# Cross-attention of a hybrid decoder trunk: the logits of heads 0 and 1 traced between the two halves of the second token tile's query projection

## The chip, the core and the metric

The kernel runs on one core of one Trainium2 chip. The metric is device time in microseconds (us) of one execution, and the median of several runs is given. The engines are named as in the profile: PE (TensorE, matmul; PEld its weight load), ACT (ScalarE), DVE (VectorE), POOL (GpSimd) and SP (SyncE, which issues the DMAs).

## What is computed

The reference is a trunk of four layers over a residual stream of 256 tokens with 1024 features. Each layer has a token mixer (convolution, dilated attention or RWKV-7), a cross-attention into 256 memory tokens with 4 heads of 256 features, and a squared-ReLU MLP; after each part comes `x = LayerNorm(alpha * x + part(x))`. The change lies in the cross-attention and in a helper that the MLP uses too:

```python
def memory_cross_attention(x, mem, w_q, w_kv, w_out):
    q = (x @ w_q).reshape(b, s, XATTN_HEADS, XATTN_HEAD_DIM)
    kv = (mem @ w_kv).reshape(b, mem.shape[1], 2, XATTN_HEADS, XATTN_HEAD_DIM)
    logits = jnp.einsum('bshe,bmhe->bhsm', q, kv[:, :, 0]) * (XATTN_HEAD_DIM ** -0.5)
    p = jax.nn.softmax(logits, axis=-1)
    o = jnp.einsum('bhsm,bmhe->bshe', p, kv[:, :, 1])
    return o.reshape(b, s, D_MODEL) @ w_out
def sq_relu_mlp(x, w1, w2):
    return jnp.square(jax.nn.relu(x @ w1)) @ w2
```

## The kernel before

Large products run as three matmuls of rounded parts. A weight chunk of 128x1024 comes by DMA from SP into `ws` (3 buffers), ACT rounds it into `wh` (a cast, L138), DVE computes the rest into `wl` (L139); `wh` and `wl` have 9 buffers each. A chunk's `ws` buffer is taken by the next DMA only when both have read it. This is `chunk`, L130 to L140. Activations are kept in the same two parts, transposed, as `xth` and `xtl`.

PSUM has three rings of 128x512 tiles: `psA` (4, L112), `psB` (2) and `psT` (2, for transposes). The 256 tokens are two tiles of 128, t = 0 and t = 1.

`xattn` (L329) runs once per layer, in four layers (0 to 3). Its steps:

- L372 loads the eight chunks of the query weights. `first_rows` (L198) multiplies token tile t with them into two `psA` tiles, the first and the second half (512 features, which are two heads each) of the queries. For t = 0 both halves advance together. For t = 1 the first half is finished, then the second: 24 matmuls each (L171).
- L378: for each half ACT copies the `psA` tile to SBUF, PE transposes it in four pieces (L213), and DVE copies the result into the per-head query tiles (L381).
- `scores(h)` (L338): four matmuls of the query tile with the keys `kt` into a `psA` tile (L343; fp32, and the profile records two matmuls for each), then DVE's maximum (L347) and scaling (L348), ACT's two exponentials (L352), DVE's reciprocal (L353) and two normalisations (L356).
- `values(h)` (L359): PE transposes the weights of the softmax, ACT copies them to SBUF (L363), four matmuls with the values `vt` go into a `psB` tile (L367), and ACT and DVE split the result into the two parts (L152, L153).
- `project` (L390) loads the eight chunks of the output weights (`x_w_out`) and multiplies; `norm` follows. The MLP's weights (`m_w`) come after these in SP's queue.

The program is traced from these calls and a scheduler then places the instructions in one queue per engine, each worked off in its order. The place in a queue is therefore not the place in the source. The MLP (L393) calls `first_rows` too, at L423, with ACT's relu and square (L425, L426) and four transposes for each half.

Of the kernel before, what the change touches and what calls it, by code (L numbers as in the profile page):

```python
# [23 lines left out]
NT = S // P  # L24
# [4 lines left out]
XH = 4  # L29
# [55 lines left out]
class Trunk:  # L85
# [112 lines left out]
    def first_rows(self, xt, t, ws):  # L198


        out = [self.A(), self.A()]
        if t == 0:
            self.gemm_tok(xt, t, ws, out)
        else:
            for j in range(2):
                self.gemm_tok(xt, t, [[a[:, j * 512:(j + 1) * 512] for a in w] for w in ws], out[j:j + 1])
        return out

    def transposes(self, src4):

# [118 lines left out]
    def xattn(self, layer, kv, xt, xt_out):  # L329
        nc, v, t_ = self.nc, self.nc.vector, self.t  # L330
        kt, vt = kv
        gb = self.load_gb(layer, 1)
        sc = XE ** -0.5
        oxt = self.xt()
        v3 = lambda a: a.rearrange("p (a b) -> p a b", a=2)
        qs, pts = {}, {}

        def scores(h):  # L338
            q = v3(qs.pop(h))
            sp = self.A()  # L340
            for t in range(NT):
                for e in range(2):
                    nc.tensor.matmul(sp[:, t * S:(t + 1) * S], q[:, e, t * P:(t + 1) * P], kt[:, 2 * h + e, :],  # L343
                                     start=e == 0, stop=e == 1)
            mx = self.sm.tile([P, 2], F32, name="mx", tag="mx")
            den = self.sm.tile([P, 2], F32, name="den", tag="den")
            v.tensor_reduce(out=mx, in_=v3(sp), axis=AX.X, op=OP.max)  # L347
            v.tensor_scalar(mx, mx, -sc, None, op0=OP.mult)  # L348
            p_ = self.g2()
            for t in range(NT):  # L350
                o = slice(t * S, (t + 1) * S)
                nc.scalar.activation(p_[:, o], sp[:, o], AF.Exp, bias=mx[:, t:t + 1], scale=sc, accum_out=den[:, t:t + 1])  # L352
            v.reciprocal(den, den)  # L353
            for t in range(NT):
                o = slice(t * S, (t + 1) * S)
                v.tensor_scalar(p_[:, o], p_[:, o], den[:, t:t + 1], None, op0=OP.mult)  # L356
            pts[h] = p_

        def values(h):  # L359
            p_ = pts.pop(h)  # L360
            pt = self.transposes([p_[:, (2 * t + m) * P:(2 * t + m + 1) * P] for m in range(NT) for t in range(NT)])
            pT = v3(self.g2())
            nc.scalar.copy(out=pT, in_=v3(pt))  # L363
            op = self.B()
            for c in range(2):
                for m in range(NT):
                    nc.tensor.matmul(op[:, c * S:(c + 1) * S], vt[:, m, (2 * h + c) * P:(2 * h + c + 1) * P],  # L367
                                     pT[:, m, :], start=m == 0, stop=m == 1)
            self.split(oxt[0][:, 2 * h:2 * h + 2, :], oxt[1][:, 2 * h:2 * h + 2, :], v3(op))

        w = t_["x_w_q"][layer]
        ws = [self.rows(w, k) for k in range(KC)]  # L372
        for h in range(XH):
            qs[h] = self.g2()
        for t in range(NT):
            for i, ps in enumerate(self.first_rows(xt, t, ws)):
                q = self.g2()
                nc.scalar.copy(out=q, in_=ps)  # L378
                pt = self.transposes([q[:, c * P:(c + 1) * P] for c in range(4)])
                for h in range(2):  # L380
                    v.tensor_copy(v3(qs[2 * i + h])[:, :, t * P:(t + 1) * P], v3(pt[:, h * 256:(h + 1) * 256]))  # L381
        scores(0)
        scores(1)
        values(0)
        scores(2)
        values(1)
        scores(3)
        values(2)
        values(3)
        self.project(oxt, t_["x_w_out"][layer], gb, xt_out)  # L390


# [1009 lines left out]
```

## Time and profile before

| | us |
|---|---|
| median of 3 runs (2051.99 to 2065.83) | 2058.36 |
| the profiled execution: its own time | 2057.95 |
| the profiled execution: its span | 2056.2 |
| PE busy in the span | 1944.8 |
| DVE busy | 1302.7 |
| ACT busy | 996.1 |

The span is what the trace covers, from the first to the last instruction; the execution's own time is 1.75 us longer. Mean granted TensorE clock: 0.972 of full speed. In timelines a row gives the start, the time, engine, line, operation, tiles and count, and in brackets the engine's idle time just before with the instruction that ended it. In the chain of waits a row gives start, time and the work that the chain ran through.

The four cross-attentions stand at about 213 to 250, 774 to 812, 1364 to 1402 and 1804 to 1841 us of the span.

### The profile page before, as it was taken

The numbers are of one execution on the slowest core, as the hardware profiler recorded it, in microseconds if no ns is written. First come the engines' busy times: TensorE is split into PE (matmuls) and PEld (weight loads), VectorE is DVE, ScalarE is ACT, GpSimd is POOL, SyncE is SP. The second block draws the span as 40 slices with busy tenths as digits, with TensorE's granted clock in tenths as the row PEclk, the third lists the DMA queues.
The fourth block names the chain that finished last, engine by engine and source line by source line (L and its number), as shares of the span: only waits on it lengthen the run. The fifth ranks groups of instructions, "written<-read, shape, count | busy, mean of one in ns | idle before, by whom it ended". The sixth has DMA issues, their size and how long they took to land.

```text
span 2056.2 us, 33010 instructions
## 1 busy us (share of the span) xinstructions
PE 1944.8 (95%) x13027; PEld 1716.0 (83%) x13027; DVE 1302.7 (63%) x2524; ACT 996.1 (48%) x1551; POOL 264.9 (13%) x160
## 2 busy tenths in 40 slices
PE   7999999998999999999999989989999898999998
PEld 7998779977999977798888777767898787878996
DVE  3986675454555564755575767776554499667544
ACT  4546445543554533555345634333555355545552
POOL 6960000000000000000011312100000663000000
PEclk9999999998999999999999989999999999999999
DMA  7644447656656533576655334344666441445662
GB/s 228 195 154 145 146 147 232 186 163 186 169 147 175 155 117 112 188 221 186 181 160 169 102 103 118 113 138 129 198 199 188 160 144 52 138 139 179 213 188 78
DMA packets 259739, 325.75 MB, mean 158 GB/s; under 512 B 25701, under 2 KB 219965, under 8 KB 259584
## 3 DMA queue, kind: packets, MB, share of 16 engines
q1 hardware_dynamic: 258432, 322.59, 50.8%
q8 instruction: 102, 1.67, 0.3%
q10 hardware_dynamic: 1152, 1.05, 0.2%
q14 instruction: 53, 0.43, 0.1%
HBM read 315.67 MB, written 6.88 MB: 157 GB/s over the span
## 4 chain that ended last, share of the span: by engine, by line
PE 68%; DVE 15%; DMA 6%; ACT 5%; issue 4%; POOL 1%; SPq 0%; DVEq 0%; ACTq 0%; POOLq 0%
PE psA L171 25%; PE psB L183 19%; PE psB L648 7%; PE psB L195 6%; DVE g L528 3%; DVE wl L139 3%; PE psT L213 3%; ACT wh L138 2%; DMA ws<-in_m_w_dram 2%; PE psB L367 2%; POOL wl L139 1%; DMA ws<-in_x_w_out_dram 1%; DVE x L269 1%; DVE bnst L270 1%; DMA ws<-in_x_w_kv_dram 1%
## 5 line engine op out<-in xcount | busy, mean ns | idle before, releaser
L138 ACT CAST wh<-ws 128x1024 fp32r<-128x1024 f32 x546 | 571.4, 1050 | 664.5 <-PE psA L171 167.0
L139 DVE TENSOR_TENSOR wl<-ws,wh 128x1024 fp32r<-128x1024 f32 (+1 forms) x462 | 568.7, 1234 | 421.4 <-ACT wh L138 418.5
L183 PE MATMUL psB<-xth,wh 128*128 128x256 f32 x1280 | 369.1, 289 | 9.4 <-ACT xth L152 3.7
L183 PE MATMUL psB<-xth,wl 128*128 128x256 f32 x1280 | 367.0, 287 | 7.7 <-DVE wl L139 7.7
L183 PE MATMUL psB<-xtl,wh 128*128 128x256 f32 x1280 | 366.6, 286 | 0.0
L183 PEld LDWEIGHTS psB<-xth,wh 128*128 128x128 f32 x1280 | 249.8, 195 | 14.0 <-ACT xth L152 4.1
L139 POOL TENSOR_TENSOR wl<-ws,wh 128x1024 fp32r<-128x1024 f32 x84 | 211.0, 2536 | 380.9 <-ACT wh L138 372.7
L183 PEld LDWEIGHTS psB<-xth,wl 128*128 128x128 f32 x1280 | 249.5, 195 | 8.9 <-DVE wl L139 8.6
L183 PEld LDWEIGHTS psB<-xtl,wh 128*128 128x128 f32 x1280 | 249.7, 195 | 2.3 <-issue 0.2
L171 PE MATMUL psA<-wh,xth 128*128 128x512 f32 x496 | 180.2, 406 | 3.5 <-ACT xth L152 3.0
L171 PE MATMUL psA<-wl,xth 128*128 128x512 f32 x496 | 177.1, 400 | 0.0
L171 PE MATMUL psA<-wh,xtl 128*128 128x512 f32 x496 | 175.9, 399 | 0.0
L171 PE MATMUL psA<-wh,hth 128*128 128x512 f32 x512 | 163.7, 396 | 0.0
L171 PE MATMUL psA<-wh,htl 128*128 128x512 f32 x512 | 163.3, 395 | 0.0
L171 PE MATMUL psA<-wl,hth 128*128 128x512 f32 x512 | 162.3, 393 | 0.0
L528 DVE SCALAR_TENSOR_TENSOR psA<-chp,ccols,psA 128x256 f32<-128x256 f32 x280 | 119.1, 481 | 3.0 <-PE psA L512 0.4
L171 PEld LDWEIGHTS psA<-wh,xth 128*128 128x128 f32 x496 | 94.8, 193 | 25.2 <-ACT xth L152 7.1
L171 PEld LDWEIGHTS psA<-wl,hth 128*128 128x128 f32 x512 | 96.5, 188 | 22.9
L171 PEld LDWEIGHTS psA<-wh,htl 128*128 128x128 f32 x512 | 96.2, 188 | 22.0
L895 POOL MEMSET rH<- 128x512 f32 x1 | 0.5, 528 | 869.6 <-DVE bnst L270 869.6
L171 PEld LDWEIGHTS psA<-wl,xth 128*128 128x128 f32 x496 | 94.9, 192 | 19.0
L171 PEld LDWEIGHTS psA<-wh,xtl 128*128 128x128 f32 x496 | 94.6, 191 | 18.9 <-DVE xtl L153 0.2
(326 smaller groups left out, 3568.2 us busy)
## 6 DMA issues: line engine op xcount, KB each, us to landing
ws<-in_m_w_dram SPq DMA_DIRECT2D x256, 512.0 KB
ws<-in_b_w_qkv_dram SPq DMA_DIRECT2D x72, 512.0 KB
ws<-in_x_w_kv_dram SPq DMA_DIRECT2D x64, 512.0 KB
ws<-in_a_w_in_dram SPq DMA_DIRECT2D x32, 512.0 KB
ws<-in_x_w_q_dram SPq DMA_DIRECT2D x32, 512.0 KB
ws<-in_x_w_out_dram SPq DMA_DIRECT2D x32, 512.0 KB
ws<-in_c_w_rkv_dram SPq DMA_DIRECT2D x24, 512.0 KB
ws<-in_a_w_out_dram SPq DMA_DIRECT2D x16, 512.0 KB
```

Source lines behind the costliest of these rows:

```text
L138: nc.scalar.copy(out=h[:rows], in_=f[:rows])
L139: self.lo_eng.tensor_tensor(l[:rows], f[:rows], h.bitcast(F32)[:rows], op=OP.subtract)
L171: nc.tensor.matmul(ps[j], l, r[:, j * 512:(j + 1) * 512], start=first and k == 0 and i == 0, stop=last and k == n - 1 and i == 2)
L183: nc.tensor.matmul(ps[:, c * S + toks.start:c * S + toks.stop], l, r, start=k == 0 and i == 0, stop=k == KC - 1 and i == 2)
L195: nc.tensor.matmul(ps[:, m * 256:(m + 1) * 256], l, r[:, k % 4, :], start=k == 0 and i == 0, stop=k == KC - 1 and i == 2)
L213: self.pe_last = self.nc.tensor.transpose(pt[:, i * P:(i + 1) * P], b, self.ident).ins
L269: v.scalar_tensor_tensor(xs, xs, ALPHA, ps[j], op0=OP.mult, op1=OP.add)
L270: v.bn_stats(st[:, j, :], xs)
L367: nc.tensor.matmul(op[:, c * S:(c + 1) * S], vt[:, m, (2 * h + c) * P:(2 * h + c + 1) * P], pT[:, m, :], start=m == 0, stop=m == 1)
L528: v.scalar_tensor_tensor(dst[:, o], hp[:, c, k:k + S], dwc(k, cc), src[:, o], op0=OP.mult, op1=OP.add)
L648: nc.tensor.matmul(ps, l[:, k, :], r[:, k, :], start=k == 0 and i == 0, stop=k == KC - 1 and i == 2)
L895: nc.gpsimd.memset(H, 0.0)
```

## The change

`first_rows` becomes a generator: for t = 1 it takes the `psA` tile of the first half, traces its matmuls and hands it out; only when the caller asks again does it trace the second half. In `xattn` the logits and the softmax of two heads, `scores(2 * i + h)`, are traced right behind the half of t = 1 that completes them, and the four `values` follow after the loop. No instruction is added or taken away.

```diff
     def first_rows(self, xt, t, ws):
-        out = [self.A(), self.A()]
         if t == 0:
+            out = [self.A(), self.A()]
             self.gemm_tok(xt, t, ws, out)
-        else:
-            for j in range(2):
-                self.gemm_tok(xt, t, [[a[:, j * 512:(j + 1) * 512] for a in w] for w in ws], out[j:j + 1])
-        return out
+            yield from out
+            return
+        for j in range(2):
+            ps = self.A()
+            self.gemm_tok(xt, t, [[a[:, j * 512:(j + 1) * 512] for a in w] for w in ws], [ps])
+            yield ps
...
                 for h in range(2):
                     v.tensor_copy(v3(qs[2 * i + h])[:, :, t * P:(t + 1) * P], v3(pt[:, h * 256:(h + 1) * 256]))
-        scores(0)
-        scores(1)
-        values(0)
-        scores(2)
-        values(1)
-        scores(3)
-        values(2)
-        values(3)
+                    if t == NT - 1:
+                        scores(2 * i + h)
+        for h in range(XH):
+            values(h)
```

In the changed file the lines from L211 to about L386 stand two higher (L343 becomes L345, L352 becomes L354, L363 becomes L365, L378 becomes L380). The orders below are those of layer 1; the tiles with a number are named by it, and `g_8209` is the softmax of head 0 before.

PE's queue, before, from the end of the second half of t = 1 (`g_8182` and `g_8191` are the two halves of the queries, `g_8060` to `g_8063` the query tiles of heads 0 to 3):

```order
L171 MATMUL psA<-wh,xtl 128x512
L213 MATMUL psT<-ident,g_8182 128x128 x4
L343 MATMUL psA<-kt,g_8060 128x256
L213 MATMUL psT<-ident,g_8191 128x128 x4
L343 MATMUL psA<-kt,g_8060 128x256 x3
L343 MATMUL psA<-kt,g_8061 128x256 x4
L343 MATMUL psA<-kt,g_8062 128x256 x4
L343 MATMUL psA<-kt,g_8063 128x256 x4
L213 MATMUL psT<-ident,g_8209 128x128 x4
L367 MATMUL psB<-g_8235,vt 128x256 x4
```

And PE's queue now, first at the end of the first half of t = 1, where the eight matmuls of heads 0 and 1 stand (the 24 matmuls of the second half follow them):

```order
L171 MATMUL psA<-wh,xtl 128x512
L345 MATMUL psA<-kt,g_8060 128x256 x2
L215 MATMUL psT<-ident,g_8157 128x128 x4
L345 MATMUL psA<-kt,g_8061 128x256 x2
L345 MATMUL psA<-kt,g_8060 128x256 x2
L345 MATMUL psA<-kt,g_8061 128x256 x2
L171 MATMUL psA<-wh,xth 128x512
```

then at the end of the second half (`g_8174`, `g_8190`, `g_8238` and `g_8254` are the softmax tiles of heads 0 to 3):

```order
L345 MATMUL psA<-kt,g_8062 128x256 x2
L215 MATMUL psT<-ident,g_8221 128x128 x4
L345 MATMUL psA<-kt,g_8063 128x256 x2
L345 MATMUL psA<-kt,g_8062 128x256 x2
L345 MATMUL psA<-kt,g_8063 128x256 x2
L215 MATMUL psT<-ident,g_8174 128x128 x4
L215 MATMUL psT<-ident,g_8190 128x128 x4
L369 MATMUL psB<-g_8265,vt 128x256 x4
L369 MATMUL psB<-g_8279,vt 128x256 x4
L215 MATMUL psT<-ident,g_8238 128x128 x4
L215 MATMUL psT<-ident,g_8254 128x128 x4
```

The same sixteen score matmuls stand in two groups of eight, and both value products of heads 0 and 1 stand together behind the last group.

ACT's queue in the same place, before, from the copy of the first half of t = 1:

```order
L378 COPY g_8182<-psA 128x512
L138 CAST wh<-ws 128x1024 x3
L378 COPY g_8191<-psA 128x512
L138 CAST wh<-ws 128x1024 x3
L352 ACTIVATE g_8209,den<-psA,mx 128x256 x2
L138 CAST wh<-ws 128x1024
L352 ACTIVATE g_8224,den<-psA,mx 128x256 x2
L138 CAST wh<-ws 128x1024
L363 COPY g_8235<-psT 128x512
```

and now:

```order
L380 COPY g_8157<-psA 128x512
L354 ACTIVATE g_8174,den<-psA,mx 128x256 x2
L354 ACTIVATE g_8190,den<-psA,mx 128x256 x2
L138 CAST wh<-ws 128x1024 x3
L380 COPY g_8221<-psA 128x512
L138 CAST wh<-ws 128x1024 x3
L354 ACTIVATE g_8238,den<-psA,mx 128x256 x2
L354 ACTIVATE g_8254,den<-psA,mx 128x256 x2
L365 COPY g_8265<-psT 128x512
L365 COPY g_8279<-psT 128x512
```

The three casts of output-weight chunks 1 to 3 stand behind the four exponentials of heads 0 and 1, and the copies for the first two value products stand behind the exponentials of heads 2 and 3. On DVE the maximum, scaling, reciprocal and normalisation of heads 0 and 1 likewise stand ahead of the three `wl` of those chunks. In layers 0 and 3 one of the second three casts stands between the two heads' exponentials, and the exponentials' table load stands ahead of head 0's. In the MLP of each layer the four transposes of the first half of t = 1 stand some matmuls further forward on PE, among those of the second half. SP's and POOL's queues keep their order but for one load of a small table.

## The prediction

> **What bounds the kernel now.** I read the page first, then the chain of waits, then PE's, ACT's and DVE's rows in one cross-attention, that of layer 1, since the change touches four such places.
>
> ```profile
> PE 1944.8 (95%) x13027; PEld 1716.0 (83%) x13027; DVE 1302.7 (63%) x2524; ACT 996.1 (48%) x1551; POOL 264.9 (13%) x160
> PE 68%; DVE 15%; DMA 6%; ACT 5%; issue 4%; POOL 1%; SPq 0%; DVEq 0%; ACTq 0%; POOLq 0%
> ```
>
> PE is busy for 95% of the span and carries 68% of the chain. The change neither adds nor removes work, so its worth is what it does to PE's idle time. PE's rows in layer 1:
>
> ```profile
> 788.32 0.60 PE L343 MATMUL psA<-kt,g 128*128 128x256 f32 x2
> 788.76 0.62 PE L213 MATMUL psT<-ident,g 128*128 128x128 f32 x4
> 789.22 6.64 PE L343 MATMUL psA<-kt,g 128*128 128x256 f32 x30
> 797.10 0.72 PE L213 MATMUL psT<-ident,g 128*128 128x128 f32 x4 [1.24 <-DVE g L356]
> 799.90 3.63 PE L367 MATMUL psB<-g,vt 128*128 128x256 f32 x8 [2.08 <-ACT g L363]
> 803.37 0.71 PE L213 MATMUL psT<-ident,g 128*128 128x128 f32 x5
> 804.87 3.62 PE L367 MATMUL psB<-g,vt 128*128 128x256 f32 x16
> ```
>
> All logits end at 789.22 + 6.64 = 795.86. PE then waits 1.24 us for head 0's softmax and 2.08 us for ACT's copy of its transposes: 3.32 us in all. A score or value record takes 6.64 / 30 = 0.22 us, so four heads' logits take 32 x 0.22 = 7.1 us and four transposes 789.22 - 788.76 = 0.46.
>
> What ends those waits is not the softmax alone. The chain of waits through the same place:
>
> ```profile
> 783.32 1.06 ACT wh L138
> 785.55 1.25 DVE wl L139 x2
> 786.80 4.98 DMA ws<-in_x_w_out_dram
> 791.86 1.05 ACT wh L138
> 794.19 4.11 DMA ws<-in_m_w_dram
> 799.27 0.59 ACT g L363
> 799.90 3.65 PE psB L367 x8
> ```
>
> The chain runs through the loading of the output weights: cast, `wl`, a DMA that needs the freed `ws` buffer, the next cast, and only then the copy that PE needs. ACT's rows show the same from its side:
>
> ```profile
> 782.70 0.59 ACT L378 COPY g<-psA 128x512 f32<-128x512 f32 x1 [5.79 <-PE psA L171]
> 783.32 2.96 ACT L138 CAST wh<-ws 128x1024 fp32r<-128x1024 f32 x3
> 789.87 1.04 ACT L138 CAST wh<-ws 128x1024 fp32r<-128x1024 f32 x1 [1.20 <-DVE g L381]
> 793.14 1.05 ACT L138 CAST wh<-ws 128x1024 fp32r<-128x1024 f32 x1 [0.23 <-DMA ws<-in_x_w_out_dram]
> ```
>
> The first three casts run at 783.32, early, while PE has 5 us of query matmuls before it. The other three wait for chunks 4 to 6.
>
> **The change in layer 1, step by step.** Durations of the small steps:
>
> ```profile
> L139 DVE TENSOR_TENSOR wl<-ws,wh 128x1024 fp32r<-128x1024 f32 x8 | 9.6, 1218 | 6.3 <-ACT wh L138 6.3
> L352 ACT ACTIVATE g<-psA,mx 128x256 f32<-128x256 f32 x8 | 3.7, 472 | 0.1
> L347 DVE TENSOR_REDUCE mx<-psA 128x2 f32<-128x512 f32 x4 | 2.7, 682 | 0.0
> L348 DVE TENSOR_SCALAR mx<-mx 128x2 f32<-128x2 f32 x4 | 0.6, 156 | 0.0
> ```
>
> - PE, first half. It ends at 782.65. Now 16 records of heads 0 and 1 and four transposes follow at once, 16 x 0.22 + 0.46 = 4.0 us, until 786.65. The transposes need ACT's copy (0.59 us), for which the two score matmuls ahead of them (four records, 0.88 us) are cover: no wait. The second half's matmuls move back by those 4.0 us and heads 2 and 3 finish again at 795.86, as the sum of work before them is the same. So far the edit costs nothing, and if that cover were gone it would cost at most the copy, 0.6 us.
> - ACT. Head 0's last record ends four records before head 1's, at 785.75; maximum and scaling (0.68 + 0.16) give 786.65, and head 1's follow by 787.5. Four exponentials at 0.47 us end at about 788.6. Only now come the three casts: 788.6 to 791.6. They ran at 783.32, so they are **5.3 us late**.
> - DVE and SP. The three `wl` and the three DMAs behind them, which need the freed buffers, move with the casts. Chunk 5 landed at 786.80 + 4.98 = 791.78; it lands now at 797.1. Chunk 6, cast at 793.14, is cast at 798.4 and done at 799.45.
> - What is queued behind: ACT takes its queue in order, and behind the last cast stand the exponentials of heads 2 and 3 (4 x 0.47 = 1.9, until 801.35) and then the copies for heads 0 and 1 (0.59), the first done at 801.9. DVE is not later: maximum of both heads by 798.6 behind the fourth `wl`, the second scaling behind one more `wl` (1.22) at 800.1, before ACT reaches head 3.
> - PE meanwhile has, after 795.86, only eight transposes of softmaxes that are long ready, 2 x 0.40 = 0.8 us, until 796.65. It then waits until 801.9: **5.2 us in place of 3.32**, so +1.9. The softmax of heads 0 and 1 is well hidden, but the wait comes back behind that of heads 2 and 3 and the late weights.
>
> Layer 2 has the same queues, and its waits before are 1.54 + 1.77 = 3.31: again +1.9.
>
> ```profile
> 1387.37 0.72 PE L213 MATMUL psT<-ident,g 128*128 128x128 f32 x4 [1.54 <-DVE g L356]
> 1389.86 3.34 PE L367 MATMUL psB<-g,vt 128*128 128x256 f32 x8 [1.77 <-ACT g L363]
> ```
>
> **Layers 0 and 3.** Their order differs a little, and they waited less:
>
> ```profile
> 237.19 0.72 PE L213 MATMUL psT<-ident,g 128*128 128x128 f32 x4 [1.35 <-DVE g L356]
> 238.51 0.61 PE L213 MATMUL psT<-ident,g 128*128 128x128 f32 x3 [0.60 <-DVE g L356]
> 1828.22 0.72 PE L213 MATMUL psT<-ident,g 128*128 128x128 f32 x4 [1.31 <-DVE g L356]
> 1829.54 0.61 PE L213 MATMUL psT<-ident,g 128*128 128x128 f32 x3 [0.60 <-DVE g L356]
> ```
>
> ```profile
> 223.56 1.06 ACT wh L138
> 228.17 4.81 DMA ws<-in_x_w_out_dram
> 234.14 1.28 ACT L352
> ```
>
> The logits ended at 237.19 - 1.35 = 235.84. In layer 1 the first half of t = 1 ended 795.86 - 782.65 = 13.2 us before that point; by the same distance it ends here at 222.6, and heads 0 and 1 are through at 226.6, where head 0 is just scaled. The table load of 1.28 us (the row at 234.14) comes first, so the exponentials run from 227.9 to 229.8 and the casts start there in place of 223.56: 6.2 late. Chunk 6 lands at 228.17 + 4.81 + 6.2 = 239.2. ACT: head 2's exponentials end at 239.55, cast 6 at 240.6, head 3's at 241.55, the first copy at 242.15. PE has its last transposes behind it at 236.95, having lost 0.25 us because DVE's query copies stand behind three late `wl`. It waits about 5.25 + 0.25 = 5.5 us where it waited 1.95 and 1.91: **+3.55 and +3.6**.
>
> In each layer the copies for heads 2 and 3 stand behind two casts; the nearest row for a wait there is 0.60 us; between that and nothing I take 0.2, four times 0.8.
>
> **The clock.** After a stretch with little PE work the granted clock halves for a time:
>
> ```profile
> 213.00:250.00 37.00, 34.67 (x171) 28.14 (x170) 23.68 (x47) 20.61 (x39) 0.00 (x0) 1.00 0.50 157
> 796.00:800.00 4.00, 0.82 (x5) 0.55 (x5) 4.00 (x13) 3.23 (x8) 0.00 (x0) 0.98 0.65 227
> 800.00:803.40 3.40, 3.40 (x9) 2.68 (x10) 1.58 (x4) 0.77 (x4) 0.00 (x0) 0.52 0.76 219
> ```
>
> Layer 1: PE was busy for 0.82 of 4.00 us, and the next 3.4 us ran at 0.52. There eight value records took 803.37 - 799.90 = 3.47 us instead of 8 x 0.22 = 1.76, so 1.7 lost. Layer 0, with 1.95 us of waits, kept 1.00. With 5.2 us without work in all four, layers 0 and 3 now pay it too: 2 x 1.7 = 3.4. Layers 1 and 2 go on paying it.
>
> [...]
>
> **The MLP** has four transposes moved forward among matmuls of the same queue. They need ACT's relu and square first, and what may hold those up is a cast in front of them, 1.05 us; the matmuls behind the transposes would wait for all of it. The other way, the splits that follow are done earlier, worth at most one ACT step such as the copy, 0.59 us. Between 0.6 gained and 1.05 lost per layer I take 0: the transposes of the query's first half, the nearest case, had no wait before them.
>
> **Sum**: 1.9 + 1.9 + 3.55 + 3.6 + 0.8 + 3.4 = 15.2 us. The profiled execution took 2057.95 (span 2056.2 and 1.75 around it), so 2073; the median of the runs is 0.4 above it. That is +0.7%.
>
> **Bounds.** If chunk 6 takes 4.11 us to land (the shortest row above), waits shrink by 0.8: 2 x 1.1 + 2 x 2.75, and without any half clock or small waits 7.7; with 4 x 0.6 gained in the MLP 5.3, so 2063. If it takes 1 us longer than 4.98, the waits grow by 1, 4 in all; with the MLP's 4 x 1.05 and one more half-clock stretch this gives 15.2 + 4 + 4.2 + 1.7 = 25, so 2083.
>
> **Rivals.** *The softmax is hidden and the waits go* (0.06): heads 0 and 1 are done while PE multiplies, so 3.32 + 3.31 + 1.95 + 1.91 = 10.5 us and both half-clock stretches, 3.2, vanish: 2044. For it: those heads' softmax really moves. Against: ACT's copies stand behind heads 2 and 3. *The wait only moves* (0.10): the transfers do not shift with the casts, and PE waits as long as before: 2058, not slower. It decides if chunk 6 lands 1.9 us (layers 1 and 2) and 3.5 us (0 and 3) earlier than worked out, within about 3 us of its issue; no landing above is shorter than 4.11. *A worse case on the same side* (0.20): two half-clock stretches around each wait, 4 x 1.7, and chunks 1 us later, 4: 15.2 + 6.8 + 4 = 26, so 2084; for it the 5 us wait is longer than a stretch of 3.4. That the scheduler undoes the change is excluded by the queues shown. My forecast has 0.64.
>
> **How the numbers follow.** One per cent, about what a measurement can tell from no change here, is 20.6 us. Even the best case gains 13.7, so faster by over 1% gets 0.02 for the unforeseen; slower by over 1% gets the worse case, 0.20, and 0.05 from the forecast's upper end; within 1% the rest, 0.73. The range takes in both bounds, the nearer half of the unmoved wait and of the worse case: 2061 to 2087.
>
> **What would show it.** Right: in each cross-attention one PE wait of about 5 us before L369 ended by ACT's copy L365, no wait ended by the softmax before the transposes of heads 0 and 1, casts of chunks 1 to 3 five to six us later against the second copy L380, and half clock after each wait in all four layers. Wrong: waits before L369 of under 3 us, a third cast that lands as early as before, or a new wait in the projection or the MLP that outweighs these.

## The result and the profile after

The changed kernel takes 2071.51 us (median of 8 runs, 2068.81 to 2076.14), the kernel before 2058.62 in runs on the same chip (8 runs, 2050.61 to 2065.83). The ratio is 1.0073, with a 95% interval of 1.0057 to 1.0088: slower, by less than one per cent. The profiled execution has a span of 2072.9 us where that of before has 2056.2, so 16.7 us more; the medians differ by 12.9.

First the same lines of the page as were shown of before, busy time and the chain's shares by engine:

```profile
PE 1947.6 (94%) x13027; PEld 1718.0 (83%) x13027; DVE 1304.4 (63%) x2524; ACT 996.1 (48%) x1551; POOL 266.2 (13%) x160
PE 68%; DVE 14%; DMA 7%; ACT 5%; issue 3%; POOL 1%; SPq 0%; DVEq 0%; ACTq 0%; POOLq 0%
```

The work is the same: PE is busy for 2.8 us more, its share falls from 95% to 94%, and the chain's shares move by one per cent at most. These lines do not show where the time went; PE's timeline does. These are the first 16 records of value matmuls in layers 0 to 3, with the wait before each in brackets:

```profile
239.45 6.72 PE L369 MATMUL psB<-g,vt 128*128 128x256 f32 x16 [5.64 <-ACT g L365]
803.39 6.35 PE L369 MATMUL psB<-g,vt 128*128 128x256 f32 x16 [4.41 <-ACT g L365]
1400.39 6.52 PE L369 MATMUL psB<-g,vt 128*128 128x256 f32 x16 [4.50 <-ACT g L365]
1843.31 5.23 PE L369 MATMUL psB<-g,vt 128*128 128x256 f32 x16 [5.29 <-ACT g L365]
```

Each cross-attention has one wait of 4.4 to 5.6 us, 19.84 in all, where the four of before had 3.32, 3.31, 1.95 and 1.91, 10.49 in all. Each is ended by ACT's copy. The 16 records took 3.62 us at full clock before; they now take 5.23 to 6.72, 10.3 us more than 4 x 3.62 (or 9.9 more than 4 x 3.72, which they take at full clock in this place in the runs below).

ACT's timeline in layer 1, from the copy of the first half to the copy that PE waits for:

```profile
784.75 0.58 ACT L380 COPY g<-psA 128x512 f32<-128x512 f32 x1 [5.81 <-PE psA L171]
788.80 0.47 ACT L354 ACTIVATE g<-psA,mx 128x256 f32<-128x256 f32 x1 [3.46 <-DVE mx L350]
...
790.61 2.95 ACT L138 CAST wh<-ws 128x1024 fp32r<-128x1024 f32 x3
794.21 0.59 ACT L380 COPY g<-psA 128x512 f32<-128x512 f32 x1 [0.65 <-PE psA L171]
796.34 1.05 ACT L138 CAST wh<-ws 128x1024 fp32r<-128x1024 f32 x1 [1.54 <-DMA ws<-in_x_w_out_dram]
798.52 1.04 ACT L138 CAST wh<-ws 128x1024 fp32r<-128x1024 f32 x1 [1.13 <-DMA ws<-in_x_w_out_dram]
799.99 1.05 ACT L138 CAST wh<-ws 128x1024 fp32r<-128x1024 f32 x1 [0.42 <-DMA ws<-in_x_w_out_dram]
...
802.74 1.08 ACT L365 COPY g<-psT 128x512 f32<-128x512 f32 x2
```

The three casts began 0.62 us after the start of the copy of the first half before (782.70 and 783.32), and now 5.86 after it. Behind them the next three casts each wait for a transfer, then come four exponentials (left out), then the copies. The chain of waits takes the same path:

```profile
790.73 0.95 ACT wh L138
...
792.84 2.37 DVE wl L139 x2
...
795.22 4.74 DMA ws<-in_x_w_out_dram
...
801.31 1.56 ACT g L354 x7
802.86 0.48 ACT g L365
...
803.39 6.37 PE psB L369 x16
```

The stretches with PE's busy time and the granted clock, in layer 1 (us, PE busy, records, clock, DMA share, GB/s):

```profile
796.00:800.00 4.00, 2.98 (x18) 1.00 0.86 267
800.00:804.00 4.00, 0.61 (x2) 0.74 0.70 225
804.00:808.00 4.00, 4.00 (x11) 0.50 0.65 197
```

The clock halves within the wait and stays halved for the first 4 us of the value matmuls and somewhat longer. In layers 0 and 3, the wait and then the value matmuls:

```profile
235.00:239.40 4.40, 0.00 (x0) 0.92 0.66 187
239.40:246.00 6.60, 6.55 (x16) 0.53 0.74 232
1838.00:1843.30 5.30, 0.02 (x1) 0.97 0.69 227
1843.30:1848.40 5.10, 5.09 (x17) 0.70 0.71 232
```

Rows of 0.1 us give the length: half clock (0.50) for 6.83 us in layers 0 to 2 (from 238.73, 801.93 and 1399.26 us on) and for 3.41 us in layer 3 (from 1842.99 on). Before it lasted 3.41 us in layers 1 and 2, and there was none in layers 0 and 3.

For comparing executions I use one more number, the length of the four cross-attentions: in each layer from the first copy of queries to the first operation of the norm. In layer 1 of the changed kernel these two rows are:

```profile
776.93 0.59 ACT L380 COPY g<-psA 128x512 f32<-128x512 f32 x1
823.99 0.69 DVE L271 SCALAR_TENSOR_TENSOR x<-x,psA 128x512 f32<-128x512 f32 x1 [8.01 <-PE psA L171]
```

That is 47.1 us; the four add up to 194.6, and before to 178.4 (44.04 + 45.22 + 45.00 + 44.10), so 16.2 more. The rest of the program, which the change does not touch apart from four transposes per layer, varies by some us from one profile to the next (1871 to 1884 us in the ten profiles here), so that this sum shows small effects better than the whole time does.

### The profile page after: what moved, and what is told of

The parts are those of the page before. It is cut to its first block, busy times and chain, and to the rows that moved or that the text cites. A ratio compares the mean times of both kernels' runs of the same rounds, so it can differ in the third digit from the quotient of the medians.

```text
span 2072.9 us, 33003 instructions
## 1 busy us (share of the span) xinstructions
PE 1947.6 (94%) x13027; PEld 1718.0 (83%) x13027; DVE 1304.4 (63%) x2524; ACT 996.1 (48%) x1551; POOL 266.2 (13%) x160
## 4 chain that ended last, share of the span: by engine, by line
PE 68%; DVE 14%; DMA 7%; ACT 5%; issue 3%; POOL 1%; SPq 0%; DVEq 0%; ACTq 0%; POOLq 0%
PE psA L171 24%; PE psB L183 19%; PE psB L646 6%; PE psB L195 6%; DVE g L526 3%; DVE wl L139 3%; PE psT L215 2%; ACT wh L138 2%; DMA ws<-in_m_w_dram 2%; PE psB L369 2%; DMA ws<-in_x_w_kv_dram 1%; DVE bnst L272 1%; POOL wl L139 1%; DVE x L271 1%; PE psA L195 1%
## 5 line engine op out<-in xcount | busy, mean ns | idle before, releaser
L171 PE MATMUL psA<-wh,xth 128*128 128x512 f32 x496 | 180.5, 406 | 3.4 <-ACT xth L152 3.3
L171 PE MATMUL psA<-wl,xth 128*128 128x512 f32 x496 | 175.3, 397 | 0.0
L171 PE MATMUL psA<-wh,xtl 128*128 128x512 f32 x496 | 174.5, 397 | 0.0
L171 PE MATMUL psA<-wh,hth 128*128 128x512 f32 x512 | 163.7, 396 | 0.0
L171 PE MATMUL psA<-wh,htl 128*128 128x512 f32 x512 | 163.3, 395 | 0.0
L171 PE MATMUL psA<-wl,hth 128*128 128x512 f32 x512 | 162.3, 393 | 0.0
L171 PEld LDWEIGHTS psA<-wl,hth 128*128 128x128 f32 x512 | 96.5, 188 | 22.9
L171 PEld LDWEIGHTS psA<-wh,htl 128*128 128x128 f32 x512 | 96.2, 188 | 22.0
L171 PEld LDWEIGHTS psA<-wh,xth 128*128 128x128 f32 x496 | 94.1, 191 | 24.3 <-ACT xth L152 6.4
L171 PEld LDWEIGHTS psA<-wl,xth 128*128 128x128 f32 x496 | 94.3, 190 | 18.9
L171 PEld LDWEIGHTS psA<-wh,xtl 128*128 128x128 f32 x496 | 93.9, 190 | 18.9 <-DVE xtl L153 0.2
```

What stands on the lines that cost most here:

```text
L171: nc.tensor.matmul(ps[j], l, r[:, j * 512:(j + 1) * 512], start=first and k == 0 and i == 0, stop=last and k == n - 1 and i == 2)
```

## The experiments

Theory, from the prediction: PE waits for ACT's copy (L365), and this stands in ACT's queue behind casts of late weights and behind the exponentials of heads 2 and 3; the half clock follows from the idle PE. What else could be: the MLP or the helper, a cause of its own in the value matmuls, or a softmax that is simply too late. All ratios are to the kernel before in runs on the same chip: its median there was 2057.20 us for the first four experiments and 2057.09 for the other four, where the first row has 2058.62, so a difference of two medians taken across the table can be off by 1.5 us; "four stages" is the sum defined above, from the one profiled execution.

| kernel | median us | ratio, 95% interval | four stages us |
|---|---|---|---|
| before | 2058.62 | | 178.4 |
| the change | 2071.51 | 1.0073, 1.0057 to 1.0088 | 194.6 |
| helper alone | 2050.84 | 0.9977, 0.9961 to 0.9994 | 171.8 |
| change, casts behind the copies | 2046.39 | 0.9948, 0.9928 to 0.9967 | 169.7 |
| change, copies before exponentials | 2053.14 | 0.9975, 0.9958 to 0.9991 | 168.6 |
| change, PE kept busy in the wait | 2064.43 | 1.0028, 1.0010 to 1.0045 | 184.3 |
| change, casts ahead of exponentials | 2066.07 | 1.0044, 1.0027 to 1.0061 | 190.3 |
| change, both orders mended | 2043.23 | 0.9932, 0.9915 to 0.9950 | 163.7 |
| before, casts behind the copies | 2038.72 | 0.9912, 0.9894 to 0.9930 | 163.8 |
| helper alone, casts behind the copies | 2040.40 | 0.9924, 0.9902 to 0.9945 | 164.2 |

### The helper alone

```diff
                     v.tensor_copy(...)
-                    if t == NT - 1:
-                        scores(2 * i + h)
-        for h in range(XH):
-            values(h)
+        scores(0)
+        scores(1)
+        values(0)
...
+        values(2)
+        values(3)
```

> Only the generator form of the query helper (so its second tile's psA is taken later, and the MLP's four transposes move among its matmuls); logits and values stay in the old order behind the loop. Theory (the MLP and the helper cost nothing, all of the loss sits in the wait before the value matmuls): the time of before, 2058 us, 2055 to 2061, with PE's waits in the cross-attentions of 2 to 3.3 us as before. Rival (part of the loss comes from the MLP's moved transposes or from the later psA tile): 2063 us or more, with the stretch from relu to norm longer in all four layers.

It was 2050.84 us: not a loss but a small gain of 0.23% over before. So the change's loss does not come from the MLP or the helper: from the MLP's relu to the first norm of the MLP the four layers take 679.9 us in the profile of before, 679.6 here and 680.9 with the change. The gain was not expected. Layer 1 shows where it lies, in ACT's rows of before and then of this kernel:

```profile
795.58 1.04 ACT L138 CAST wh<-ws 128x1024 fp32r<-128x1024 f32 x1 [0.23 <-DMA ws<-in_x_w_out_dram]
...
798.32 1.05 ACT L138 CAST wh<-ws 128x1024 fp32r<-128x1024 f32 x1 [0.77 <-DMA ws<-in_m_w_dram]
799.27 0.58 ACT L363 COPY g<-psT 128x512 f32<-128x512 f32 x1
```

```profile
795.19 1.04 ACT L138 CAST wh<-ws 128x1024 fp32r<-128x1024 f32 x1
796.13 0.59 ACT L365 COPY g<-psT 128x512 f32<-128x512 f32 x1
```

Before, one more cast, of an MLP weight that waits for its transfer, stands ahead of the copy. Without it the copy starts 14.88 us after the copy of the first half (781.25) in place of 16.57. PE's wait in layer 1 is 1.42 us in place of 3.32, and the half clock is gone: eight value records take 1.99 us there in place of 3.63. Why the queue came out with one cast fewer was not traced further. But it says that the waits of before hang on casts too.

### Casts behind the copies

An edge queues ACT's casts of the output weights, from chunk 3 on (counted from 0, the fourth of eight), behind the copy for head 1. Nothing else is moved by hand.

```diff
-            nc.scalar.copy(out=pT, in_=v3(pt))
+            cp[h] = nc.scalar.copy(out=pT, in_=v3(pt)).ins
...
-        ws = [self.rows(w, k) for k in range(KC)]
+        ws = [self.rows(w, k) for k in range(KC if behind is None else 3)]
+        if behind is not None:
+            with self.tc.issue_after(behind):
+                ws += [self.rows(w, k) for k in range(3, KC)]
```

(`behind` is `cp[1]`, passed by `xattn`; the convolution's `project` passes none.)

> The changed kernel, but ACT's casts of the output weights from chunk 4 on are queued behind the copy of head 1's transposed softmax. Theory (late chunks, whose casts stand ahead of the exponentials of heads 2 and 3 and of the copies, make PE wait): in layer 1 logits end at 798.0, maximum and scaling of head 3 by 798.85, exponentials by 799.8, first copy done by 800.4, so the wait shrinks from 4.41 to about 1.5 us; over four layers the waits go from 19.84 (5.64 + 4.41 + 4.50 + 5.29) to about 6.2, and the value matmuls, at 6.72, 6.35, 6.52 and 5.23 us where 3.62 is full clock, lose their half clock (10.3 us): 2071.5 - 13.6 - 10.3 = 2048 us, 2044 to 2056. Rival A (the softmax of heads 2 and 3 alone holds the copies, casts do not matter): waits of 4 us or more, 2068 to 2072. Rival B (the casts put back make the projection wait instead): waits before the value matmuls of 1.5, but new ones before the projection's matmuls, 2058 or more.

It was 2046.39 us, 25.1 less than the change, as the theory had it. ACT's rows in layer 1, from the exponentials of heads 2 and 3, and PE's wait behind them:

```profile
795.63 0.47 ACT L357 ACTIVATE g<-psA,mx 128x256 f32<-128x256 f32 x1 [3.49 <-DVE mx L353]
...
797.44 1.08 ACT L368 COPY g<-psT 128x512 f32<-128x512 f32 x2
798.38 2.03 ACT L138 CAST wh<-ws 128x1024 fp32r<-128x1024 f32 x2
```

```profile
798.09 3.72 PE L372 MATMUL psB<-g,vt 128*128 128x256 f32 x16 [1.77 <-ACT g L368]
```

ACT now waits 3.49 us for head 2's maximum, so it is idle where it stood waiting for transfers; the copies follow the exponentials at once. The wait is 1.77 us, in all four layers alike, and the 16 records take 3.72 us. The two rivals are out: the softmax of heads 2 and 3 accounts for 1.77 of 4.4 to 5.6 us, and no new wait appeared in the projection.

### Copies before exponentials

Here the casts stay, and the exponentials of heads 2 and 3 are queued behind the copies for heads 0 and 1 (`scores` is split into logits and `softmax`, `values` into `turn`, the transposes and the copy, and the rest).

```diff
+        turn(0)
+        turn(1)
+        with self.tc.issue_after(cp[1]):
+            softmax(2)
+            softmax(3)
+        values(0)
+        values(1)
```

> The changed kernel with the same order on PE, but ACT's exponentials of heads 2 and 3 are queued behind the copies for heads 0 and 1; the casts of the output weights may stay ahead of those. Theory (the copies wait for the whole of ACT's queue, casts and exponentials): the copies come right behind PE's transposes (798.98 in layer 1) or behind a cast of 1.05 us, waits of 0.5 to 1.5 us in place of 4.4 to 5.6 and no half clock: 2071.5 - 15.8 - 10.3 = 2045 us, 2041 to 2054. Rival A (the late chunks of weights alone decide, with their casts still ahead of the copies): waits of 3 us or more, 2064 to 2072. Rival B (the exponentials of heads 2 and 3 are now late in their turn): the wait moves behind the first eight value matmuls, 2058 or more.

```profile
797.78 1.04 ACT L138 CAST wh<-ws 128x1024 fp32r<-128x1024 f32 x1 [1.37 <-DMA ws<-in_x_w_out_dram]
798.73 1.07 ACT L369 COPY g<-psT 128x512 f32<-128x512 f32 x2
```

```profile
799.36 3.72 PE L376 MATMUL psB<-g,vt 128*128 128x256 f32 x16 [1.31 <-ACT g L369]
```

The waits are 0.79, 1.31, 1.24 and 0.92 us (in layers 0 and 3 before head 1's product, since head 0's copy comes earlier there), with a cast right ahead of the copy, and the value matmuls take 3.72 us for 16 records, or 1.89 and 1.99 for eight each, as at full clock. The stages sum to 168.6, 26.0 less than the change. The median, 2053.14, lies in the expected range but 8 us above the 2045 worked out; the profile has 1881 us outside the cross-attentions, against 1874 with the casts behind. Why that part was longer was not found out.

So the wait has no single owner. ACT takes the copies only when the casts, held up by transfers, and the exponentials behind them are all done, and moving either of the two out of their way takes off most of it: without the casts the exponentials run as soon as the maxima are there, and without the exponentials the copies follow a cast that has come in.

### PE kept busy in the wait

```diff
+        def fill(h, n):
+            ops[h] = self.B()
+            with self.tc.issue_after(self.pe_last):
+                for _ in range(n):
+                    nc.tensor.matmul(ops[h][:, :S], kt[:, 0, :P], kt[:, 1, :], start=True, stop=True)
...
+        turn(0)
+        turn(1)
+        fill(0, 10)
+        values(0)
+        values(1)
```

> The changed kernel with ten extra matmuls (keys by keys, 128x256, two records of 0.22 us each, 4.4 us in all) on PE between the transposes of head 1 and the value matmuls of head 0, written to a psB tile that the value matmuls then overwrite. They add work only while PE waits. Theory (the wait of 4.4 to 5.6 us has its own price, and the half clock behind it a second one, which goes with PE's idleness): value matmuls of heads 0 and 1 at 3.6 us in place of 6.72, 6.35, 6.52 and 5.23, start of the value matmuls unmoved: 2071.5 - 10.3 = 2061 us, 2058 to 2065. Rival A (the value matmuls are slow for another cause, their operands or the copies): 2071 or more. Rival B (the extra matmuls push the value matmuls back): 2073 or more.

PE's rows in layers 1 and 0:

```profile
799.25 4.48 PE L371 MATMUL psB<-kt 128*128 128x256 f32 x20
803.81 3.72 PE L378 MATMUL psB<-g,vt 128*128 128x256 f32 x16
```

```profile
236.58 4.48 PE L371 MATMUL psB<-kt 128*128 128x256 f32 x20
242.13 3.72 PE L378 MATMUL psB<-g,vt 128*128 128x256 f32 x16 [1.07 <-ACT g L365]
```

The value matmuls start as late as they did (in layer 1, 5.44 us after the transposes for heads 0 and 1 began, 803.81 - 798.37, and 803.39 - 797.94 = 5.45 in the change; within 0.3 us in the other layers), and take 3.72 in each layer. The granted clock of the stretch around layer 1's cross-attention is 1.00, where the change has 0.91 (the row of this kernel, then of the change):

```profile
777.00:817.00 40.00, 39.86 (x194) 1.00 0.34 112
```

```profile
776.00:816.00 40.00, 35.53 (x164) 0.91 0.36 119
```

The stages sum to 184.3, 10.3 less than the change, of which 9.9 lie in these value matmuls (24.82 us in the four layers then, 14.88 now); the median is 7.1 less. So the half clock is a price of its own, beside the wait, and it goes with PE's idleness and not with the operands.

### Casts ahead of exponentials

The prediction had said that the three casts are late because they stand behind the exponentials of heads 0 and 1. Here the first four output-weight chunks are traced before the logits, and those exponentials are queued behind their casts.

```diff
+                if t == NT - 1 and i == 0:
+                    wo = [self.rows(t_["x_w_out"][layer], k) for k in range(4)]
+                    cast = self.cast
...
+            with self.tc.issue_after(cast):
+                for t in range(NT):
...
```

> The changed kernel, but the exponentials of heads 0 and 1 are queued on ACT behind the first four casts of output weights, so that these casts no longer stand behind exponentials. Theory A (that of the prediction: the three casts are late because they stand behind the exponentials): in layer 1 they start right behind ACT's copy, at about 785.4 in place of 790.6, the later chunks land 5 us earlier, and the waits before the value matmuls go from 4.4 to 5.6 us to under 0.5 each, the half clock with them: about 2043 us, 2039 to 2049. Theory B (the casts are late because their wh buffers still hold query weights, which the second half's matmuls, now 4 us later, must read first: nine buffers, eight of them query weights): ACT waits for PE, the casts run at about 789.3, 790.3 and 791.3, only 1.2 us earlier, and the waits shrink by about 1.2 us each, 4.8 in all, and by up to one half-clock stretch each: 2060 to 2067 us.

It was 2066.07 us, theory B. ACT's rows in layer 1:

```profile
783.34 0.58 ACT L384 COPY g<-psA 128x512 f32<-128x512 f32 x1 [5.81 <-PE psA L171]
787.97 2.95 ACT L138 CAST wh<-ws 128x1024 fp32r<-128x1024 f32 x3 [4.04 <-PE psA L171]
790.83 0.46 ACT L355 ACTIVATE g<-psA,mx 128x256 f32<-128x256 f32 x1
```

With nothing ahead of it in the queue, the first cast still waits 4.04 us, and what ends the wait is a query matmul of PE (L171). `wh` has nine buffers; eight hold query weights and one the first output chunk, so the next cast needs a buffer that the second half's matmuls must have read, and the change puts 4 us of logits and transposes ahead of these. The casts start 4.63 us after the copy, against 5.86 with the change and 0.62 before. So there are two conditions, and the later one counts: the buffers alone hold the casts back by 4.0 us, and the exponentials ahead of them, which end 1.2 us after the buffers are free, by 5.2. Without the exponentials only the 1.2 are won. What the casts would do with free buffers was not run; in the change ACT's row shows them right behind the exponentials, which had waited 3.46 us for the maximum of head 0. The waits fell only to 3.43, 4.30, 4.81 and 3.43 us: in layers 1 and 2 nothing was gained, since an eighth cast (at 799.37) now stands between the exponentials and ahead of the copies.

### Both orders mended, and the same edit without the change

The two edges together; then the casts' edge alone on the kernel before, and on the helper alone. The edits are those shown above.

> The changed kernel with the same order on PE; on ACT both the exponentials of heads 2 and 3 and the casts of the output weights from the fourth on are queued behind the copies for heads 0 and 1. Theory (each of the two alone left a wait: 1.77 us with the exponentials still ahead, 0.8 to 1.3 with the casts still ahead): no wait over 0.5 us before the value matmuls, four times 1.77 us less than with the casts alone put back: 2046.4 - 7.1 = 2039 us, 2035 to 2045. Rival (the casts or the later exponentials then make PE wait further on, at the values of heads 2 and 3 or in the projection): 2046 or more.

> The kernel before, with nothing changed but that ACT's casts of the output weights from the fourth on are queued behind the copy of head 1's transposed softmax. Theory (the waits of before came from the same queue: the copy for head 0, at 799.27 in layer 1, stands behind a cast that waits for a weight transfer): the waits of 3.32, 3.31, 1.95 and 1.91 us go down to 0.5 or less each and the half clock of layers 1 and 2 goes: 2058.6 - 8.5 - 3.2 = 2047 us, 2043 to 2051. Rival (the softmax of heads 0 and 1 itself sets these waits): 2056 or more.

> The generator form of the helper with logits and values in the old order, and ACT's casts of the output weights from the fourth on queued behind the copy of head 1's transposed softmax. Theory: its waits of 1.57, 1.42, 1.70 and 1.04 us go to 0.5 or less: 2050.8 - 4 = 2047 us, 2042 to 2050, the same as the kernel before with that one edit, and slower than the moved logits with both orders mended (2039) if moving the logits brings cover of its own. Rival (moving the logits brings nothing once the queue is right): the same time as that kernel within 2 us.

Both edges on the change, in layer 1 (ACT, then PE):

```profile
791.79 1.07 ACT L372 COPY g<-psT 128x512 f32<-128x512 f32 x2 [3.83 <-PE psT L215]
```

```profile
792.43 3.72 PE L379 MATMUL psB<-g,vt 128*128 128x256 f32 x16 [0.29 <-ACT g L372]
```

Now ACT waits for PE. PE's wait is 0.29 us, the end of head 0's copy, in all four layers. The kernel before with the casts' edge, PE and ACT in layer 1:

```profile
791.60 1.03 PE L346 MATMUL psA<-kt,g 128*128 128x256 f32 x4
792.49 1.99 PE L370 MATMUL psB<-g,vt 128*128 128x256 f32 x8
794.32 0.60 PE L213 MATMUL psT<-ident,g 128*128 128x128 f32 x4
```

```profile
791.85 0.58 ACT L366 COPY g<-psT 128x512 f32<-128x512 f32 x1 [0.42 <-PE psT L213]
795.50 2.94 ACT L138 CAST wh<-ws 128x1024 fp32r<-128x1024 f32 x3
```

The last logits and the first values follow each other without a wait, and the casts run 3.65 us later than the copy. The stages sum to 163.7, 163.8 and 164.2: the three orders of logits and values come to the same length once the casts are out of the way. The best median, 2038.72, is that of the kernel before with the one edge, 0.88% under before; its interval overlaps those of the two others, so by them the three are not told apart. If one differs, it is the change with both edges: its six runs (2040.89 to 2046.02) hardly overlap those of the best (2036.67 to 2043.42), and the stages show no reason for it. Both edges on the change came out 4 us above the expectation, the other two 8 and 7 us below: I had left them 2 us of waits, and there were none of that size (0.17 and 0.18 us, in layers 0 and 3). The stages fell by 14.5 and 7.7 us, 2.8 and 3.9 more than these two forecasts had; the rest is outside the stages and was not explained. The rival of the third run holds: moving the logits brings no cover that the old order lacked.

## Why the prediction was right, and where not

The time (2073 foretold, 2071.5 measured) and the likeliest case came out, and so did the place of the wait: one per cross-attention, before the first value matmuls, ended by ACT's copy, with the half clock behind it in all four layers. Step by step:

- **PE's first half at no cost**: right. No transposes of queries wait, and in layers 0 and 3 DVE's query copies cost 0.15 us of the 0.25 foretold.
- **The casts, five to six us late**: right in time. With the 2.05 us by which layer 1 starts later in this execution, they were due at 790.65 and began at 790.61; in layer 0 ACT's table load (1.28 us, at 223.30) stands ahead of the exponentials, as foretold. The reason given ("Only now come the three casts", behind the exponentials) holds, but it is one of two: the `wh` buffers that the query weights still hold, which the forecast left out, would by themselves have kept the casts back by 4.0 us. The number came out because the later of the two counts and that one, later by 1.2 us, was the one priced.
- **Chunks, casts, exponentials, copies**: right in order. The first copy was due at 803.95 (801.9 + 2.05) and ended at about 803.3. The transfers were some tenths of a us quicker than those of before that the forecast went by (the one in the chain took 4.74), so the copy came 0.6 earlier, and PE's transposes ended 0.3 later, at 798.98 against 796.65 + 2.05: the wait is 4.41 and 4.50 in layers 1 and 2 and not 5.2. The transfers did shift with the casts (the last one in the chain was issued at 795.22 and landed at 799.96), so the rival in which the wait only moves, at no loss, is out. In layers 0 and 3 the wait is 5.64 and 5.29, each with 0.15 more before the transposes, for 5.5. The waits grew by 9.65 us in all against 10.95.
- **Small waits for heads 2 and 3**, 0.8: none appeared.
- **The half clock**, 3.4: this term was mis-sized. It was taken as one stretch of 1.7 us in each layer, 6.6 in all with layers 1 and 2 as before. The value matmuls lost 3.1, 2.7, 2.9 and 1.6 us, 10.3 in all, so 7.1 more than before. The half clock lasted two stretches (6.83 us) in three of the layers, which was a part of the worse rival, and one (3.41 us) in layer 3. The run with PE kept busy shows the loss by itself: 10.3 us in the stages, 9.9 of them in the value matmuls.
- **The MLP at nothing**: right within 1 us: 680.9 us in the four layers against 679.9, and the helper alone lost nothing there.
- The sum of what was measured is 9.65 + 7.1 = 16.75, beside 16.2 in the stages and the 15.2 of the prediction: the waits were 1.3 too long and the small waits 0.8 too many, the clock 3.7 too cheap. That these errors partly cancel is luck, and so is a median within 1.5 us of 2073: by the profiles the change costs 16.7 us, by the medians 12.9.
- The rival in which the waits vanish was rightly refused for this change, and for the reason given, the copies' place behind the rest of ACT's queue: with this place mended they do vanish, at 2043 us.

## What to carry to other kernels

In ACT's queue here the copies that PE waited for were as late as the transfers that earlier steps waited for: in layer 1 of the changed kernel the last of these landed at 799.96, and the copies began at 802.74, behind its cast and four exponentials. Look for the casts of the next weights ahead of such a step before you move matmuls to hide a softmax. Here one edge that queues those casts behind the copies gave 0.9%, and the moved logits gave nothing beside it. When a block of work is moved ahead of a large product, ask also whose buffers that product releases: here some 4 us of logits and transposes were put ahead of it, and in the run with the casts ahead of the exponentials the first cast waited 4.04 us for one of its matmuls.

## What the runs showed of the hardware

- After one wait of 4.4 to 5.6 us PE ran at half clock (0.50) for 6.83 or 3.41 us, and the loss did not grow with the wait: 16 value records took 6.35 us after a wait of 4.41, and 5.23 after one of 5.29. After the waits of 1.77 us, with the casts behind the copies, the clock stayed at 1.00 in all four layers. In layer 1 of before, with two waits of 1.24 and 2.08 us, it was 0.50 for 3.41 us from 799.85 on; in layer 0 of before, with 1.35 and 0.60, it stayed at 1.00.
- In the profiled executions of the changed kernel and of before the clock changed on a grid. The four drops of the changed kernel lie 563.20, 597.33 and 443.73 us apart, which is 165, 175 and 130 times 3.4133, and in 606 stretches of 3.4133 us, cut on both sides of 801.93, the clock of each is 1.00 or 0.50 and nothing between (the same in 602 stretches of the kernel before, cut on both sides of 799.85). What a wait cost in the four layers went with where it lay on this grid: in layer 3 it reached 0.3 us past the drop, and the clock came back after one stretch; in layers 0, 1 and 2 it reached 0.7, 1.5 and 1.1 us past it, and the clock came back after two.
- With matmuls whose result nobody reads, 4.48 us of them in the wait, the clock was 1.00 around all four cross-attentions, where it was 0.91 to 0.96 without them, and the four stages were 10.3 us shorter. That is a remedy for the clock alone: the wait stayed, and the kernel stayed slower than before (1.0028).
